# Four Strassen units instead of three in two column pairs of a decoder trunk

## The chip, the cores and the metric

The kernel runs on one core of a Trainium2 chip. The metric is device time in microseconds. The core has TensorE (PE) for matmuls, VectorE (DVE), ScalarE (ACT), GpSimd (POOL) and SyncE (SP), which issues nearly all DMAs. Each engine works through its own instructions in a fixed order and waits on the others through semaphores.

## The reference

One layer of a decoder trunk over 256 tokens of width 2048, all in fp32. It is nine large projections with element-wise work and a short recurrence between them:

```
u = rmsnorm(x) @ W_in               # 2048 -> 12288: c, b, xa, za, q, f, iv, og (1024 each), ga, gb (2048 each)
ya = b * conv3(c * xa) * silu(za)
yb = rmsnorm(hgrn2(silu(q), f, iv)) * silu(og)      # gated linear recurrence, 8 heads of 128
m = sigmoid(ga) * (ya @ W_a) + sigmoid(gb) * (yb @ W_b)
x = x + m @ W_o                                     # 2048 -> 2048
x = x + sigmoid(rmsnorm(x) @ W_pg) * (p @ W_pp)     # 2048 -> 2048
out = rmsnorm(x)
```

## The kernel before

**Splits.** A matmul in full precision is made of three in a faster rounded format (fp32r): each operand is the sum of a rounded part "hi" and the rest "lo", and hi·hi + hi·lo + lo·hi is accumulated. The weights are streamed from memory. For each part of 128 rows x 1024 columns of the stream, SP loads `raw` (`load_raw`, three buffers of two parts, 1 MB each), ACT writes `whi` = raw rounded (L166) and DVE `wlo` = raw − whi (L167). This is `split`. So ACT, DVE and PE each pass over the whole weight stream once. The activations are the stationary operand: for each 128 rows of them and each half of the tokens PE loads 128x128 and streams 512 columns of weights.

**Groups, pairs and programs.** A column group is 512 columns wide. Most groups run alone, in eight steps of two 128-row blocks; a step is 12 matmuls. Six pairs of groups run together by a program, a list of units `(u, c)`, where `c` names a chunk of 256 rows of the contraction. `(0, c)` or `(1, c)` is two chunks of one group, `(2, c)` one chunk of both: two parts, 24 matmuls. `("S", c)` is one chunk of both groups by a Strassen scheme, seven products instead of eight: 21 matmuls. It has four parts, three of 1024 columns and one of 512. Behind its part 0, `combine_weights` makes sums and differences of the weights on DVE: L181 (128x1024), L184 and L185 (128x512). Part 1 is the split of the 512-wide sum `t2`. The activations need sums of their own, the forms (`forms`, L777 to L785), made earlier: those of the second half's pair by `forms_of_x` out of a fresh load of x, those of the last gate pair in `ep_o`, behind the transposition of x.

The pairs that matter here are `VG` (program `INNER`: value `iv` and output gate `og` of the second half of the heads) and `GP` (program `LATE`: the second and third group of W_pg). `OUT` is the program of the first two groups of W_o; the third and fourth run alone as `O` (j = 2, 3). Then come the first W_pg group (`PG`, 0), `GP`, and the last one (`PG`, 3).

**What sets the order.** The program is written step by step, and each engine keeps the order in which its instructions were written, except that a scheduler may move one forward by its own estimate of times. `tc.issue_after` forbids this: an instruction under it stays behind the named one on its engine. The main loop splits ahead of PE by `ahead(pos)` parts: three, some more where extra buffers are open (`MORE`), and up to five more in the tail. In between it runs the epilogues, generators that do one piece of work at each `yield` (`advance`, `step`); the pieces stand behind the last splits (`state["splits"]`). In the ranges `inner` and `tied` the splits too stand behind the last split.

**Transpositions.** `turned` turns a block of 256 tokens x 512 columns: four DMAs write it to memory (`turn`, L346), one reads it back (L350), and after `lag` yields DVE transposes its 32x32 squares (L354). `ep_o` does so with each 512 columns of x: an addition of the matmul's result (L845), two copies on ACT (L947), the DMAs, the squares for the norm (L954), the transposition, and for j ≥ 2 four `put` (L310 on ACT and L311 on DVE, hi and lo of the turned block). PE needs the blocks in the first W_pg group: the last one, j = 3, in its seventh step. `ep_f` makes the recurrence's decay of one half of the heads: two sigmoids on ACT (L400, L402), four operations of DVE on 256 columns (L407), four more for the keys (L414), logarithms on ACT that need a table load (L424), a scan on DVE (L434). Its second half runs beside `VG`.

PSUM has banks of two sets, "g" and "s"; `bank` takes the next of a set.

Of the kernel before, what the change touches and what calls it, by code (L numbers as in the profile page):

```python
# [10 lines left out]
F32R = mybir.dt.float32r  # L11
# [4 lines left out]
P = 128  # L16
T = 256
# [23 lines left out]

GATES = ("S", 0), (0, 2), ("S", 1), (1, 2), ("S", 4), (0, 6), ("S", 5), (1, 6)
OPENING = (0, 2), (0, 4), ("S", 0), (0, 6), ("S", 1), (1, 2), (1, 4), (1, 6)
INNER = (0, 4), ("S", 0), (0, 6), ("S", 1), (2, 3), ("S", 2), (1, 4), (1, 6)
FRONT = (0, 2), (0, 4), (0, 6), ("S", 0), (1, 2), ("S", 1), (1, 4), (1, 6)
OUT = (0, 4), ("S", 0), (1, 4), ("S", 1), (2, 3), ("S", 2), (0, 6), (1, 6)
LATE = (0, 4), ("S", 0), (0, 6), ("S", 1), (2, 3), ("S", 2), (1, 4), (1, 6)


PRM_GMIX, PRM_GPLE, PRM_GHG, PRM_LB, PRM_CONV = 0, 16, 32, 40, 48  # L50
# [5 lines left out]
def hybrid_kernel(ctx, tc, xT, x, pT, prm, gfin, masks, w_in, w_a, w_b, w_o, w_pg, w_pp, out):  # L56
# [195 lines left out]
    closing = last_unit("OO", OUT)  # L252
    last = range(gates[-1] + 1, closing + 1)
    outer = range(closing + 6, of_kind("O")[-1] + 1)
    tied.append(range(last[0] - 4, outer[-1] + 1))
    inner = [of_kind(kind) for kind in ("QV", "VG")]
    inner = range(inner[0][0] - 3, inner[0][-1] + 1), range(inner[1][0] - 6, inner[1][-1] + 1)

# [44 lines left out]
    def put(op, k, src, scale=None):  # L303

        hi, lo = op[0][:, k, :], op[1][:, k, :]
        if scale is None:
            nc.scalar.activation(out=hi, in_=src, func=AF.Copy)
            nc.vector.tensor_tensor(out=lo, in0=src, in1=hi.bitcast(F32), op=ALU.subtract)
        else:
            nc.scalar.activation(out=hi, in_=src, func=AF.Identity, scale=scale)  # L310
            nc.vector.scalar_tensor_tensor(  # L311
                out=lo, in0=src, scalar=scale, in1=hi.bitcast(F32), op0=ALU.mult, op1=ALU.subtract
            )


    def rsqrt_of(ss, n, width, tag):
# [20 lines left out]
    def turned(src, lag, dst=None):  # L337

        d = dram.tile([P, 4, T], F32, tag="turn", bufs=3, name=nm("turn"))
        to = d.rearrange("(b i) a x -> a i b x", b=4)
        for a in range(4):
            state["sent"] = nc.sync.dma_start(  # L346
                out=to[a], in_=src[32 * a : 32 * a + 32, :].rearrange("i (b x) -> i b x", b=4)
            ).ins
        yield
        nc.sync.dma_start(out=src, in_=d.rearrange("p a x -> p (a x)"))  # L350
        for _ in range(lag):
            yield
        dst = t4() if dst is None else dst
        nc.vector.transpose(  # L354
            out=dst.rearrange("p (k a e) -> p a k e", a=4, e=32), in_=src.rearrange("p (a k e) -> p a k e", a=4, e=32)
        )
        return dst
# [37 lines left out]
    def ep_f(j, psum):  # L395
# [8 lines left out]
        one, low = (state[n][:, j * 4 : j * 4 + 4] for n in ("oml", "lbm"))  # L404
        for h in range(4):
            s = slice(h * T, (h + 1) * T)
            nc.vector.tensor_scalar(  # L407
                out=sg[:, s], in0=sg[:, s], scalar1=one[:, h : h + 1], scalar2=low[:, h : h + 1],
                op0=ALU.mult, op1=ALU.add,
            )  # L410
# [5 lines left out]
            )  # L416
        yield
        yield


        lf, last = t4(), sc(8, "lfl", 2)
        lv, fv = segments(lf), segments(sg)
# [518 lines left out]
    def ep_o(j, psum):  # L941
        xs = state["x"]
        x1 = t4()
        for t in range(NT):
            d = xs[:, t, j * CW : (j + 1) * CW]
            add(d, d, psum[t])
            nc.scalar.activation(out=spread(x1, t), in_=blocks(d), func=AF.Copy)  # L947
        turn = turned(x1, 6 if j == 1 else 2)
        next(turn)
        yield  # L950
        junk = t4()
# [18 lines left out]
            yield from forms("x1T", form_tiles(pools["tmp3"], f"So{j}", len(chunks)), r, chunks)  # L970
            return
        for c in range(4):
            put(state["x1T"], j * 4 + c, x1[:, c * T : (c + 1) * T], gain(PRM_GPLE, j * 4 + c))
        if j == 3:
            tot = sc(2, "tot2", 1)
            nc.vector.tensor_reduce(
# [342 lines left out]
    for pos, (gi, c) in enumerate(steps[:last_group]):  # L1319
# [31 lines left out]
            step(active[-1])  # L1351
        if pos == inner[1][0] - 8:
            third = [
                pools["branch"].tile([P, 1024], F32R, tag=f"ybT{x}1", bufs=1, name=nm("form"))[:, :512] for x in "hl"
            ]
            active.append(forms_of_x((2,), lambda n: lambda: third))
            step(active[-1])
        if 0 <= pos - NORM < 4:
            add_squares(pos - NORM)
# [40 lines left out]
                load_projection(1 + c[0] // 2)  # L1400
            continue
        if c == 0:
            psum = [bank("s" if kind == "PP" and j > 1 else "g") for _ in range(NT)]
        hi, lo = parts.pop(pos)
        for i in range(2):
            k = 2 * c + i
# [134 lines left out]
```

## Time and profile before

| | |
|---|---|
| median of 3 runs | 807.91 us (807.77 to 809.03) |
| the profiled execution | 809.07 us, its span 807.3 |
| PE busy | 798.0 us, 99% |
| DVE busy | 685.1 us, 85% |
| ACT busy | 492.1 us, 61% |
| POOL busy | 95.4 us, 12% |
| DMA | 191.20 MB, mean 237 GB/s |
| PE's clock | 0.9 or more of full speed in all slices but the last |

The trace is of one execution. A row of a timeline gives the start in us from the span's start, the duration (of the whole run of instructions, where there are several: x3), the engine, the line, the operation, output and inputs without buffer numbers, and in brackets how long the engine had been idle and what ended it. A matmul's row is longer than the time it holds PE, because matmuls overlap; what counts is from start to start. "Ready" of a part is the end of its L167.

In the kernel after the change the lines from ep_f on are numbered up to seven higher: L354 becomes L355, L407's place on ACT is L409, L947 becomes L954, L954 becomes L961, L1017 becomes L1024, L1258 and L1280 become L1265 and L1287.

### The profile page before, as it was taken

To read this page: it belongs to the slowest core of one execution; us is meant where nothing else is said; L and a number is where in the kernel's file an instruction comes from. 1 tells how busy PE (TensorE), PEld (TensorE's weight loads), DVE (VectorE), ACT (ScalarE), POOL (GpSimd) and SP (SyncE) were. 2 spreads that over 40 slices of the span, in tenths; PEclk is the share of its full clock that TensorE was granted. 3 is DMA by queue.
4 is the path that set the end of the run, shared out by engine and by line. 5 is a ranking of instruction groups with operands and counts; after the bars stand their busy time and mean duration, and the time that the engine had idled before them with its cause. 6 is when DMAs were issued, how large, how long until landed. Compare 5 with 4: busy or idle time off the path is not lost.

```text
span 807.3 us, 11113 instructions
## 1 busy us (share of the span) xinstructions
PE 798.0 (99%) x4169; PEld 662.3 (82%) x4169; DVE 685.1 (85%) x798; ACT 492.1 (61%) x662; POOL 95.4 (12%) x74
## 2 busy tenths in 40 slices
PE   9999999999999999999999999999999999999995
PEld 7888888888888888888888888888888888887885
DVE  5968897966779987978998998998998988859995
ACT  6967565575656665586674564564565556746562
POOL 0000145300000054300001000000100000002032
PEclk9999999999999999999999999999999999999998
DMA  9899855747676755667584775775875669877542
GB/s 345 295 335 319 268 174 203 237 167 241 240 261 190 261 183 201 209 211 257 189 307 158 227 275 171 239 264 179 275 266 196 208 246 348 327 236 281 205 173 104
DMA packets 50309, 191.20 MB, mean 237 GB/s; under 512 B 5712, under 2 KB 15184, under 8 KB 36304
## 3 DMA queue, kind: packets, MB, share of 16 engines
q1 hardware_dynamic: 50112, 190.24, 68.4%
q8 instruction: 32, 0.52, 0.2%
q10 hardware_dynamic: 144, 0.26, 0.1%
q14 instruction: 21, 0.17, 0.1%
HBM read 175.80 MB, written 14.68 MB: 236 GB/s over the span
## 4 chain that ended last, share of the span: by engine, by line
PE 82%; DVE 10%; issue 2%; DMA 2%; ACT 2%; SPq 0%; POOL 0%; ACTq 0%; POOLq 0%; DVEq 0%
PE g L1258 48%; PE g L1280 25%; PE s L1280 6%; DVE wlo L167 5%; DMA raw<-in_w_pg 2%; ACT whi L166 1%; DVE raw L181 1%; DMA raw<-in_w_o 1%; PE s L1258 1%; PE s L504 1%; DVE t L845 1%; PE s L1131 1%; DVE t L184 1%; DVE t L1017 0%; DVE t L354 0%
## 5 line engine op out<-in xcount | busy, mean ns | idle before, releaser
L167 DVE TENSOR_TENSOR wlo<-raw,whi 128x1024 fp32r<-128x1024 f32 (+1 forms) x320 | 390.2, 1243 | 92.2 <-ACT whi L166 89.4
L166 ACT ACTIVATE whi<-raw 128x1024 fp32r<-128x1024 f32 (+1 forms) x320 | 325.8, 1047 | 175.8 <-PE g L1258 98.3
L1258 PE MATMUL g<-whi,xl 128*128 128x512 f32 (+1 forms) x464 | 177.1, 382 | 0.3 <-DVE xl L311 0.3
L1258 PE MATMUL g<-whi,xh 128*128 128x512 f32 (+1 forms) x464 | 177.4, 383 | 0.0
L1258 PE MATMUL g<-wlo,xh 128*128 128x512 f32 (+1 forms) x464 | 177.1, 382 | 0.0
L1280 PE MATMUL g<-whi,xl 128*128 128x512 f32 x316 | 122.9, 389 | 0.0
L1280 PE MATMUL g<-wlo,xh 128*128 128x512 f32 x316 | 122.9, 389 | 0.0
L1280 PE MATMUL g<-whi,xh 128*128 128x512 f32 x316 | 122.6, 389 | 0.0
L1258 PEld LDWEIGHTS g<-whi,xl 128*128 128x128 f32 x464 | 87.2, 188 | 17.6 <-DVE xl L311 0.8
L1258 PEld LDWEIGHTS g<-whi,xh 128*128 128x128 f32 x464 | 87.2, 188 | 17.0 <-ACT xh L310 0.3
L1258 PEld LDWEIGHTS g<-wlo,xh 128*128 128x128 f32 x464 | 87.3, 188 | 16.8
L166 ACT ACTIVATE whi<-t 128x512 fp32r<-128x512 f32 x25 | 15.8, 632 | 92.1 <-DVE t L184 92.1
L1280 PEld LDWEIGHTS g<-whi,xl 128*128 128x128 f32 x316 | 59.3, 188 | 12.4
L1280 PEld LDWEIGHTS g<-whi,xh 128*128 128x128 f32 x316 | 59.3, 188 | 12.3
L1280 PEld LDWEIGHTS g<-wlo,xh 128*128 128x128 f32 x316 | 59.3, 188 | 12.3
L927 POOL TENSOR_TENSOR t<-ga,gb 128x512 f32<-128x512 f32 x6 | 10.6, 1790 | 188.0 <-issue 118.1
L181 DVE TENSOR_TENSOR raw<-raw 128x1024 f32<-128x1024 f32 x25 | 31.5, 1261 | 0.6
L1258 PE MATMUL g<-whi,yaTh 128*128 128x512 f32 (+1 forms) x74 | 28.2, 388 | 0.0
L1258 PE MATMUL g<-wlo,yaTh 128*128 128x512 f32 (+1 forms) x74 | 27.9, 383 | 0.0
L1258 PE MATMUL g<-whi,yaTl 128*128 128x512 f32 (+1 forms) x74 | 27.9, 383 | 0.0
L1258 PE MATMUL g<-whi,mh 128*128 128x512 f32 x64 | 24.8, 391 | 0.1
L1258 PE MATMUL g<-whi,ml 128*128 128x512 f32 x64 | 24.9, 389 | 0.0
(309 smaller groups left out, 1117.0 us busy)
## 6 DMA issues: line engine op xcount, KB each, us to landing
raw<-in_w_in SPq DMA_DIRECT2D x68, 1024.0 KB, 5.0
raw<-in_w_in SPq DMA_DIRECT2D x37, 512.0 KB, 5.1
raw<-in_w_o SPq DMA_DIRECT2D x12, 1024.0 KB, 6.5
raw<-in_w_pg SPq DMA_DIRECT2D x12, 1024.0 KB, 6.4
raw<-in_w_in SPq DMA_DIRECT2D x38, 256.0 KB, 5.1
turn<-t SPq DMA_DIRECT2D x72, 128.0 KB, 2.8
t<-turn SPq DMA_DIRECT2D x18, 512.0 KB, 5.2
raw<-in_w_a SPq DMA_DIRECT2D x8, 1024.0 KB, 5.6
```

The costliest lines, as they stand in the source:

```text
L166: a = nc.scalar.activation(out=hi[:, s], in_=src[:, s], func=AF.Copy)
L167: v = nc.vector.tensor_tensor(out=lo[:, s], in0=src[:, s], in1=hi[:, s].bitcast(F32), op=ALU.subtract)
L181: nc.vector.tensor_tensor(out=b[:, 0:4:3, :], in0=b[:, 0:3:2, :], in1=b[:, 3:4, :].to_broadcast([P, 2, CW]), op=ALU.subtract)
L184: nc.vector.tensor_tensor(out=t2, in0=b[:, 2, :], in1=b[:, 0, :], op=ALU.add)
L504: nc.tensor.matmul(heads(bk)[r, h, c if at is None else slice(at, at + 32)], key(h)[:, r], query(h)[:, c], start=True, stop=True, tile_pos ...
L845: nc.vector.tensor_tensor(out=out, in0=x, in1=y, op=ALU.add)
L927: (nc.vector if j == 3 else nc.gpsimd).tensor_tensor(out=spread(m, t), in0=blocks(ga[:, s]), in1=blocks(gb[:, s]), op=ALU.add)
L1131: nc.tensor.matmul(wb[:m, :n], *ones, start=True, stop=True)
L1258: nc.tensor.matmul(psum, a, b, start=first and n == 0, stop=last and n == 2)
L1280: nc.tensor.matmul(banks[name], x, y[:, s], start=k == total[name] and i == 0, stop=k == 1 and i == 2)
```

## The change

```diff
-INNER = (0, 4), ("S", 0), (0, 6), ("S", 1), (2, 3), ("S", 2), (1, 4), (1, 6)
+INNER = (0, 4), ("S", 0), (0, 6), ("S", 1), (1, 4), ("S", 2), ("S", 3), (1, 6)
-LATE = (0, 4), ("S", 0), (0, 6), ("S", 1), (2, 3), ("S", 2), (1, 4), (1, 6)
+LATE = (0, 4), ("S", 0), (0, 6), ("S", 1), (1, 4), ("S", 2), ("S", 3), (1, 6)
...
-    tied.append(range(last[0] - 4, outer[-1] + 1))
+    tied.append(range(last[0] - 4, late + 10))
...
     def put(op, k, src, scale=None):
-            nc.scalar.activation(out=hi, in_=src, func=AF.Identity, scale=scale)
-            nc.vector.scalar_tensor_tensor(
+            a = nc.scalar.activation(out=hi, in_=src, func=AF.Identity, scale=scale)
+            v = nc.vector.scalar_tensor_tensor(
...
+            return a.ins, v.ins
...
     def ep_f(j, psum):
         for h in range(4):
             s = slice(h * T, (h + 1) * T)
+            if j:
+                nc.scalar.activation(
+                    out=sg[:, s], in_=sg[:, s], func=AF.Identity, scale=one[:, h : h + 1], bias=low[:, h : h + 1]
+                )
+                continue
             nc.vector.tensor_scalar(
...
         yield
         yield
+        if j:
+            yield
...
     def ep_o(j, psum):
-        turn = turned(x1, 6 if j == 1 else 2)
+        turn = turned(x1, (2, 6, 6, 4)[j])
...
-            put(state["x1T"], j * 4 + c, x1[:, c * T : (c + 1) * T], gain(PRM_GPLE, j * 4 + c))
+            state["splits"] = put(state["x1T"], j * 4 + c, x1[:, c * T : (c + 1) * T], gain(PRM_GPLE, j * 4 + c))
...
-                pools["branch"].tile([P, 1024], F32R, tag=f"ybT{x}1", bufs=1, name=nm("form"))[:, :512] for x in "hl"
+                pools["branch"].tile([P, 1024], F32R, tag=f"ybT{x}1", bufs=1, name=nm("form")) for x in "hl"
             ]
-            active.append(forms_of_x((2,), lambda n: lambda: third))
+            active.append(forms_of_x((2, 3), lambda n: lambda: third))
...
-            psum = [bank("s" if kind == "PP" and j > 1 else "g") for _ in range(NT)]
+            psum = [bank("s" if kind == "PP" and j > 1 or kind == "O" and j == 2 else "g") for _ in range(NT)]
```

1. In `INNER` and `LATE` the unit `(2, 3)` becomes `("S", 3)`. It stands directly behind `("S", 2)`, and `(1, 4)` moves ahead of both. Everywhere in the kernel before a Strassen unit has another kind of unit ahead of it.
2. The forms for chunk 3: `forms_of_x` makes two chunks at once, and the forms of the second quarter of x in `ep_o` (j = 1) become 1024 wide, since `chunks` there is read from `LATE`.
3. In `ep_f`, for the second half, the four L407 become activations on ACT, and the logarithms come one step later.
4. The transpositions of x wait 2, 6, 6 and 4 steps (before: 2, 6, 2, 2); the four `put` of j = 2 and 3 become part of `state["splits"]`, and the tied range reaches ten parts into the first W_pg group. So the splits there stand behind the puts, and in written order.
5. The third W_o group takes banks of the set "s".

On DVE, in VG, from the end of the unit `(2, 3)` over S2 on (`raw_2355` is S2's tile, `wlo_2433` its part 0). Before:

```order
L167 TENSOR_TENSOR wlo_2433<-raw_2355,whi_2432 128x1024
L181 TENSOR_TENSOR raw_2355<-raw_2355 128x2x512
L184 TENSOR_TENSOR t_416_2436<-raw_2355 128x512
L185 TENSOR_TENSOR raw_2355<-raw_2355,t_416_2436 128x512
L167 TENSOR_TENSOR wlo_2446<-t_416_2436,whi_2445 128x512
L167 TENSOR_TENSOR wlo_2456<-raw_2355,whi_2455 128x1024
L167 TENSOR_TENSOR wlo_2466<-raw_2355,whi_2465 128x1024
L167 TENSOR_TENSOR wlo_2482<-raw_2419,whi_2481 128x1024
L167 TENSOR_TENSOR wlo_2501<-raw_2419,whi_2500 128x1024
L167 TENSOR_TENSOR wlo_2511<-raw_2443,whi_2510 128x1024
```

After, with S2's tile `raw_2357` and S3's `raw_2421`:

```order
L167 TENSOR_TENSOR wlo_2437<-raw_2357,whi_2436 128x1024
L181 TENSOR_TENSOR raw_2357<-raw_2357 128x2x512
L184 TENSOR_TENSOR t_416_2440<-raw_2357 128x512
L185 TENSOR_TENSOR raw_2357<-raw_2357,t_416_2440 128x512
L167 TENSOR_TENSOR wlo_2450<-t_416_2440,whi_2449 128x512
L167 TENSOR_TENSOR wlo_2460<-raw_2357,whi_2459 128x1024
L167 TENSOR_TENSOR wlo_2470<-raw_2357,whi_2469 128x1024
L167 TENSOR_TENSOR wlo_2487<-raw_2421,whi_2486 128x1024
L181 TENSOR_TENSOR raw_2421<-raw_2421 128x2x512
L184 TENSOR_TENSOR t_427_2490<-raw_2421 128x512
L185 TENSOR_TENSOR raw_2421<-raw_2421,t_427_2490 128x512
L167 TENSOR_TENSOR wlo_2509<-t_427_2490,whi_2508 128x512
```

Three splits of parts stand between the two blocks of additions. In GP the same happens, save that part 3 is split ahead of part 1.

On ACT, where the last quarter of x is copied for its transposition (the copies are L947 before, L954 after; the squares L954, then L961). Before:

```order
L166 ACTIVATE whi_6288<-raw_6158 128x1024
L310 ACTIVATE xh_5825<-t_1103_6183,prm_t 128x256 x4
L947 ACTIVATE t_1114_6273<-xs 128x4x4x32
L954 ACTIVATE t_1120_6306,ss_1036_5822<-xs 128x512
L947 ACTIVATE t_1114_6273<-xs 128x4x4x32
L954 ACTIVATE t_1120_6306,ss_1036_5822<-xs 128x512
L166 ACTIVATE whi_6310<-raw_6237 128x1024
L166 ACTIVATE whi_6328<-raw_6237 128x1024
```

After:

```order
L310 ACTIVATE xh_5838<-t_1115_6258,prm_t 128x256 x4
L166 ACTIVATE whi_6268<-raw_6171 128x1024
L166 ACTIVATE whi_6301<-raw_6171 128x1024
L166 ACTIVATE whi_6323<-raw_6240 128x1024
L166 ACTIVATE whi_6341<-raw_6240 128x1024
L954 ACTIVATE t_1119_6286<-xs 128x4x4x32 x2
L961 ACTIVATE t_1125_6319,ss_1041_5835<-xs 128x512 x2
L166 ACTIVATE whi_6357<-raw_6284 128x1024
```

Four splits moved ahead of the copies. On SP's queue at the same place, where `turn` is that quarter on its way out and the load with `turn` as its source its way back. Before:

```order
L346 DMA turn_6278<-t_1114_6273 32x4x256 x4
L131 DMA raw_6326<-in_w_pg 128x2048
L350 DMA t_1114_6273<-turn_6278 128x1024
L119 DMA raw_6376<-in_w_pg 128x1024
L121 DMA raw_6376<-in_w_pg 128x512 x2
L1209 DMA pw_6396<-kept_224 128x1024
```

After:

```order
L1216 DMA pw_6409<-kept_224 128x1024
L131 DMA raw_6339<-in_w_pg 128x2048
L347 DMA turn_6291<-t_1119_6286 32x4x256 x4
L119 DMA raw_6373<-in_w_pg 128x1024
L121 DMA raw_6373<-in_w_pg 128x512
L351 DMA t_1119_6286<-turn_6291 128x1024
L121 DMA raw_6373<-in_w_pg 128x512
```

A load of 1 MB moved ahead of the four transfers, and most of the next tile's load ahead of the way back.

## The prediction

> **What bounds the kernel.** I read the page's first part, then the waits of PE, then the timelines of PE and DVE around the two pairs whose program changes.
>
> ```profile
> PE 798.0 (99%) x4169; PEld 662.3 (82%) x4169; DVE 685.1 (85%) x798; ACT 492.1 (61%) x662; POOL 95.4 (12%) x74
> ```
>
> ```profile
> PE g L1258 <- DVE xl L311: 0.3, 1, 0.3
> ```
>
> PE is the bound: it is busy 99% of a span of 807.3 us, and the waits view shows one wait of 0.3 us for another engine. So time can go only with matmuls, or come with new waits on split weights. The waits view hides small ones, because a row of PE lasts 0.39 us and rows overlap; a wait shows as a start that comes more than 0.227 us after the last one. That pitch is read below between 267.14 and 267.37. Three places have more.
>
> The first is inside S2 of the second half's pair (VG). These are PE's starts there, and DVE's rows:
>
> ```profile
> 266.01 0.39 PE L1280 MATMUL s<-wlo,xh 128*128 128x512 f32 x1
> 267.14 0.39 PE L1280 MATMUL s<-whi,form 128*128 128x512 f32 x1
> 267.37 0.39 PE L1280 MATMUL s<-wlo,form 128*128 128x512 f32 x1
> 268.05 0.39 PE L1280 MATMUL g<-whi,xh 128*128 128x512 f32 x1
> 268.46 0.50 PE L1280 MATMUL g<-whi,form 128*128 128x512 f32 x1
> 268.80 0.39 PE L1280 MATMUL s<-whi,form 128*128 128x512 f32 x1
> ```
>
> ```profile
> 261.26 2.32 DVE L167 TENSOR_TENSOR wlo<-raw,whi 128x1024 fp32r<-128x1024 f32 x2
> 263.61 1.22 DVE L181 TENSOR_TENSOR raw<-raw 128x1024 f32<-128x1024 f32 x1
> 264.87 0.69 DVE L184 TENSOR_TENSOR t<-raw 128x512 f32<-128x512 f32 x1
> 265.59 0.69 DVE L185 TENSOR_TENSOR raw<-raw,t 128x512 f32<-128x512 f32 x1
> 266.34 0.69 DVE L167 TENSOR_TENSOR wlo<-t,whi 128x512 fp32r<-128x512 f32 x1
> 267.50 5.76 DVE L167 TENSOR_TENSOR wlo<-raw,whi 128x1024 fp32r<-128x1024 f32 x5 [0.46 <-ACT whi L166]
> ```
>
> 268.05 to 268.46 is 0.41 and 268.46 to 268.80 is 0.34, so S2 loses 0.18 + 0.11 = 0.29 us. The reader is to see why: S2's part 0 is ready at 263.58 (261.26 + 2.32), 2.43 us ahead of its use at 266.01; part 1 is ready at 267.03 and used at 267.37, 0.34 ahead. The three additions of a Strassen unit have eaten the lead. The second and third places come with their parts below.
>
> **Six Strassen products fewer.** VG and the last gate pair (GP) each swap a unit of 24 matmuls for one of 21: 3 x 0.227 = 0.68 us less of PE in each, 1.36 in all. This is certain, as PE has no idle time that would take it back.
>
> **VG, the price of two neighbours.** Each Strassen unit now has DVE's three additions behind its part 0, and no plain unit stands between S2 and S3. From S2's part 0 to S3's part 0 DVE needs: additions and the half split, 263.58 to 267.03, 3.45; the whole split behind ACT, to 267.50 + 1.15 = 268.65, 1.62 to 1.70; two more at 1.15 (5.76 / 5). That is 7.4 us for a unit that PE eats in 21 x 0.227 = 4.76. To S3's part 1 it is 7.4 + 3.45 = 10.85 us, and PE wants that part 21 + 6 matmuls after S2's part 0, 6.12 us. The lead falls by 4.73; there are 2.43 us of it, plus what the rest of the change gives ahead of S2. Part 2 is then late by 0.37 more: it follows part 1 by 1.70 on DVE, by 1.33 on PE once S2's 0.29 is taken off (part 2's lo is used at about 269.0).
>
> What the change gives ahead of S2 is the four L407 operations moved to ACT.
>
> ```profile
> 236.85 0.41 DVE L407 TENSOR_SCALAR t<-t,lc,lc 128x256 f32<-128x256 f32 x1
> 237.18 1.22 DVE L181 TENSOR_TENSOR raw<-raw 128x1024 f32<-128x1024 f32 x1
> 247.05 3.50 DVE L167 TENSOR_TENSOR wlo<-raw,whi 128x1024 fp32r<-128x1024 f32 x3 [1.36 <-ACT whi L166]
> 243.52 1.28 ACT L424 ACT_TABLE_LOAD   x1
> 713.59 1.71 ACT L310 ACTIVATE xh<-t,prm_t 128x256 fp32r<-128x256 f32 x4
> ```
>
> One costs DVE 0.33 (236.85 to 237.18), four 1.3: that is the upper end of the gain. The lower end is nothing, as DVE already waits 1.36 at 247.05 for ACT, which has loaded a table (1.28) between two splits, and ACT now has four instructions more ahead of that. Following both rows of instructions, ACT's four (estimated at 0.43 each, 1.71 / 4, from the same form in the tail) hold the half split of S0 back by 0.6, and the table load still stands ahead of the fifth split. I find S2's part 0 ready 0.4 earlier, nearer the lower end, and take 0.4. So VG stalls 4.73 - 2.43 - 0.4 + 0.37 = 2.3 us; net, with S2's 0.29 gone and 0.68 fewer: 2.3 - 0.29 - 0.68 = **+1.3** (bounds: 0.4 with the whole 1.3, 1.7 with nothing). The plain unit and the epilogues behind it refill the lead.
>
> The wider form (one DMA more, forms of 1024 instead of 512) costs DVE a split of 1.22 instead of 0.69 and four additions twice as wide, some 1 us by the rows above, and ACT as much. It lies some 10 us ahead of this row:
>
> ```profile
> 232.21 2.36 DVE L167 TENSOR_TENSOR wlo<-raw,whi 128x1024 fp32r<-128x1024 f32 x2 [4.90 <-ACT whi L166]
> ```
>
> DVE stands idle for 4.90 in one go before VG, so I cost it at nothing. If that cover were gone, it would come off the lead of S2. The wider form in the output groups is costed the same way.
>
> **The bank of O's third group.** Its first matmul waits for a bank of the set that the pair ahead of it still occupies.
>
> ```profile
> 669.12 0.39 PE L1258 MATMUL g<-whi,ml 128*128 128x512 f32 x1
> 669.58 0.50 PE L1258 MATMUL g<-whi,mh 128*128 128x512 f32 x1
> ```
>
> 0.46 instead of 0.23, and 0.11 behind it: 0.34 us. The other set of banks is free by then. I take **-0.34** (between 0 and that).
>
> **The tail.** Call T0 the first matmul of the first w_pg group (712.55). In it PE loses time where it needs the last quarter of x, transposed:
>
> ```profile
> 712.55 0.39 PE L1258 MATMUL g<-whi,xh 128*128 128x512 f32 x1
> 730.46 0.39 PE L1280 MATMUL g<-wlo,xh 128*128 128x512 f32 x1
> 730.78 0.50 PE L1258 MATMUL g<-whi,xh 128*128 128x512 f32 x1
> 731.12 0.39 PE L1258 MATMUL g<-wlo,xh 128*128 128x512 f32 x1
> 732.04 0.40 PE L1280 MATMUL g<-whi,xh 128*128 128x512 f32 x1
> 732.79 0.73 PE L1258 MATMUL g<-whi,xl 128*128 128x512 f32 x2 [0.35 <-DVE xl L311]
> ```
>
> 0.09 + 0.11 + 0.52 and 0.11 behind the last: 0.83 us. The order now puts that quarter's transposition (L355) and the four L311 ahead of two splits on DVE, but its copies out of x behind four splits on ACT, and its four transfers behind a load of 1 MB on SP's queue. Before, its chain ran so:
>
> ```profile
> 715.21 0.62 ACT L947 ACTIVATE t<-xs 128x512 f32<-128x512 f32 x1
> 717.60 3.90 ACT L166 ACTIVATE whi<-raw 128x1024 fp32r<-128x1024 f32 x4
> L346 SPq DMA_DIRECT2D turn<-t x4: 325/438/446, 717.1 to 718.4; - x4
> 722.24 0.34 SPq L350 DMA_DIRECT2D t<-turn  x1
> 728.86 1.24 DVE L354 STREAM_TRANSPOSE t<-t 128x1024 f32<-128x1024 f32 x1
> DMA to landing us min/median/max: 2.1/3.8/5.6
> raw<-in_w_pg SPq DMA_DIRECT2D x12, 1024.0 KB, 6.4
> ```
>
> In the new order three splits run from T0 (3 x 0.98), the copies take 1.1, so the transfers start at T0 + 4.1 and the last is issued at 5.5 (before, the first at 717.1, T0 + 4.6, and the last at 718.4). Landing takes 3.8 as before (718.4 to 722.24), then 5.6 back: X, the start of the transposition, is T0 + 15.0 (before T0 + 16.31). Bounds: 13.7, with the shortest and the median landing, and 16.3, no better than before. PE needs the quarter at T0 + 16.3; a transposition of 1.2 and the first of four conversions fit to within some tenths.
>
> From X on DVE never waits long, and its rows add up. Before:
>
> ```profile
> 745.23 2.20 DVE L181 TENSOR_TENSOR raw<-raw 128x1024 f32<-128x1024 f32 x1
> 747.47 1.67 DVE L184 TENSOR_TENSOR t<-raw 128x512 f32<-128x512 f32 x1
> 751.52 4.62 DVE L167 TENSOR_TENSOR wlo<-raw,whi 128x1024 fp32r<-128x1024 f32 x4
> 742.48 6.10 POOL L1026 TENSOR_TENSOR xs<-xs,gfin_t 128x512 f32<-128x512 f32 x2 [18.46 <-ACT t L1019]
> 761.24 0.39 PE L1280 MATMUL s<-wlo,xh 128*128 128x512 f32 x1
> ```
>
> S2's part 0 is ready at 751.52 + 4.62 = 756.14, 27.28 after the transposition; the new order has one split more between: 28.4. Then S2 to S3's part 0, 7.35 (as in VG), and to S3's part 2, whose split stands behind that of part 3, 1.25 + 0.72 + 0.61 + 1.14 + 0.60 + 1.14 = 5.5: X + 41.2, or T0 + 56.2. PE, without waits, would use S2's part 0 at 761.24 - 0.83 = T0 + 47.86, S3's 4.76 later, and its part 2 nine matmuls (2.04) on: T0 + 54.66. PE is 1.6 us late in all by then (0 at X = 13.4; 2.9 at 16.3). Net: 1.6 - 0.83 - 0.68 = **+0.1**. Behind S3 the plain units give DVE its lead back.
>
> The 41.2 holds two additions that ran long while POOL worked: 2.20 and 1.67 against 1.22 and 0.69 in VG, 1.96 in all. The Trainium skill, SBUF — State Buffer, "Who interferes with whom", says that a VectorE instruction with two SBUF inputs and a GpSimd one that reads SBUF take one port as a lock, and that the later one blocks for the whole instruction. By that rule up to 2 x 3.05 us would go, 4.1 more than the rows show. The rows show 0.98 each, and the sum goes by them.
>
> **Sum.** 1.3 - 0.34 + 0.1 = +1.1 us. The profiled execution took 809.07 (span 807.3 and what lies around it), the median of the runs is 807.91; the sum is a difference, and set on the median it gives 809.0. Its own bounds are 806.5 (VG 0.4, tail -1.5, bank -0.34: -1.4) and 811.0 (VG 1.7, tail 1.4, bank 0: +3.1). I count 0.2%, 1.6 us, as what can be told from no change.
>
> **Rivals.**
> *A, the lead holds.* If ACT's delays ahead of S2 fall away and DVE is more than 1 us further ahead in VG, and X is early, only savings stay: -1.36 - 0.29 - 0.34 - 0.83 = -2.8, 805.1; with one small stall 805.9. For it: DVE is busy 85% of the span, and waits 1.36 and 0.46 in rows above that a better order could fill. Against: the 10.85 of DVE against 6.12 of PE leaves 2.3 us to find. Chance 0.24.
> *B, the last quarter comes later.* Its four transfers now stand behind a load of 1 MB, and each us on X is a us of the end. From X = T0 + 15.6 on the kernel is slower by over 1.6; at 17.0 it is +3.1, 811.0. For it: the load would be issued at about T0 + 3.2, when the second split frees its buffer, and such a load takes 6.4 by the row above; transfers that move only behind it land at 9.6 or later, and 5.6 back make X 15.2 to 16. Against: they are ready 0.5 earlier than before. The Trainium skill, DMA: Bandwidth & Descriptors, "Queues, rings and completion order", has each ring consumed in order, which is this rival's mechanism; no run yet shows these transfers behind a load. Chance 0.22.
> *C, POOL's two products block whole instructions of DVE.* In the new order they start beside splits instead of additions; at 3.05 us each (6.10 / 2) they cost 4.1 more: 813.1. The rows above speak against it. Chance 0.05.
> *D, one of the two stalls only.* S3 stalls in VG but not in the tail: 1.3 - 0.34 - 1.5 = -0.5, 807.4. Chance 0.04.
>
> **How the numbers follow.** The forecast has 0.45, of which a quarter (0.12) lies above 809.5 and the rest within. Faster: A, 0.24. Slower: 0.12 + B 0.22 + C 0.05 = 0.39. Same: 0.33 + D 0.04 = 0.37. The range reaches down to A with a small stall, 805.6, and up beyond B, 812.0; what lies outside is the best part of A and C. The forecast's own range is 806.5 to 811.0.
>
> **What would show it.** PE rows: 6 matmuls fewer, a start 1.5 to 2 us late at S3's part 1 in VG with DVE's half split as releaser, none at S2. DVE: two blocks of additions with three splits between, no wait longer than 0.5 in the second. No 0.46 at the third O group. In the tail the transposition at T0 + 14 to 16, a late start of PE in S3 of GP. The prediction fails if VG's S3 waits less than 1 us (my 0.4 was too small), or if X is outside 13.7 to 16.3.

## The result

The changed kernel takes 817.03 us (815.85 to 817.27), the kernel before in the same runs 808.05 (807.77 to 809.03): a ratio of 1.0103, 95% interval 1.0091 to 1.0115. The forecast was 809.0, no change that can be told, with a range up to 812.0; the result lies outside. The profiled execution has a span of 815.5 us, 8.2 more than before.

The waits of PE, after (us in total, times, longest):

```profile
PE g L1265 <- ACT xh L310: 3.1, 1, 3.1
PE s L1287 <- ACT whi L166: 1.1, 1, 1.1
...
PE g L1265 <- DVE t L852: 0.4, 1, 0.4
PE g L1265 <- DVE v L852: 0.4, 1, 0.4
...
PE s L1287 <- DVE wlo L167: 0.2, 1, 0.2
```

There are three kinds. The second and the last of these rows are S3 of the second half's pair. Its PE and DVE timelines:

```profile
271.96 0.39 PE L1287 MATMUL g<-whi,xl 128*128 128x512 f32 x1
273.46 0.49 PE L1287 MATMUL s<-whi,form 128*128 128x512 f32 x1 [1.11 <-ACT whi L166]
274.19 0.50 PE L1287 MATMUL s<-wlo,form 128*128 128x512 f32 x1 [0.23 <-DVE wlo L167]
274.99 0.39 PE L1287 MATMUL g<-whi,xh 128*128 128x512 f32 x1
275.55 0.50 PE L1287 MATMUL g<-whi,form 128*128 128x512 f32 x1 [0.16 <-ACT whi L166]
```

```profile
262.05 1.21 DVE L167 TENSOR_TENSOR wlo<-raw,whi 128x1024 fp32r<-128x1024 f32 x1
...
267.18 3.50 DVE L167 TENSOR_TENSOR wlo<-raw,whi 128x1024 fp32r<-128x1024 f32 x3 [0.46 <-ACT whi L166]
270.71 1.23 DVE L181 TENSOR_TENSOR raw<-raw 128x1024 f32<-128x1024 f32 x1
...
273.44 0.69 DVE L167 TENSOR_TENSOR wlo<-t,whi 128x512 fp32r<-128x512 f32 x1
```

From start to start, less 0.227 each, S3 loses 1.27 + 0.50 + 0.11 + 0.33 + 0.11 = 2.32 us. Part 0 of S2 is ready at 263.26, 0.32 earlier than before; as PE's starts stand 0.28 later in this trace (its use is at 266.29, before at 266.01), the lead over PE is 3.03 instead of 2.43. Part 1 of S3 is ready at 274.13, 10.87 behind part 0 of S2. S2's own 0.29 us are gone, and so is the wait at the third W_o group.

The second kind waits for a bank. The group behind each of the two pairs writes a bank that the pair's last additions (L852) have to empty first:

```profile
285.20 0.39 PE L1265 MATMUL g<-whi,xl 128*128 128x512 f32 x1
286.00 0.50 PE L1265 MATMUL g<-whi,xh 128*128 128x512 f32 x1 [0.41 <-DVE v L852]
783.22 0.39 PE L1287 MATMUL g<-whi,xl 128*128 128x512 f32 x1
784.05 0.50 PE L1265 MATMUL g<-whi,xh 128*128 128x512 f32 x1 [0.45 <-DVE t L852]
```

0.57 + 0.11 and 0.61 + 0.11: 0.68 and 0.72 us. Neither is in the trace of before.

The third and largest is where PE needs the last quarter of x, in the first W_pg group. T0 is now 714.54.

```profile
730.64 0.39 PE L1265 MATMUL g<-whi,xl 128*128 128x512 f32 x1
734.15 0.80 PE L1265 MATMUL g<-whi,xh 128*128 128x512 f32 x1 [3.12 <-ACT xh L310]
734.75 0.63 PE L1265 MATMUL g<-wlo,xh 128*128 128x512 f32 x1
735.17 0.63 PE L1265 MATMUL g<-whi,xl 128*128 128x512 f32 x1
```

PE stands still for 3.29 us more than its pitch, and then its pitch is 0.43 instead of 0.227. The windows of PE (length, busy with its count, granted clock, DMA share, GB/s) show why; the granted clock is the share of full speed at which TensorE runs:

```profile
715.00:730.00 15.00, 15.00 (x68) 1.00 0.73 242
730.00:734.00 4.00, 1.03 (x5) 0.94 0.98 354
734.00:740.00 6.00, 5.85 (x14) 0.50 0.41 140
740.00:745.00 5.00, 5.00 (x23) 0.96 0.54 197
```

The trace's clock record has 0.50 from 733.5 to 740.4, 6.8 us, of which PE has work in 6.2. The wait (with 0.37 behind its first matmul) is 3.65, the slow matmuls cost 13 x 0.2 = 2.6: PE is 6.3 us late by 740. In the gate pair no Strassen unit waits any more.

The quarter's chain, in the order of its steps:

```profile
713.95 1.71 ACT L310 ACTIVATE xh<-t,prm_t 128x256 fp32r<-128x256 f32 x4 [2.63 <-DVE t L355]
715.57 3.89 ACT L166 ACTIVATE whi<-raw 128x1024 fp32r<-128x1024 f32 x4
719.36 1.14 ACT L954 ACTIVATE t<-xs 128x512 f32<-128x512 f32 x2
720.23 0.33 SPq L131 DMA_DIRECT2D raw<-in_w_pg  x1
720.60 2.40 SPq L347 DMA_DIRECT2D turn<-t  x4
728.18 0.33 SPq L351 DMA_DIRECT2D t<-turn  x1
732.31 1.25 DVE L355 STREAM_TRANSPOSE t<-t 128x1024 f32<-128x1024 f32 x1 [6.96 <-DMA t<-turn]
```

ACT stood idle 2.63 us for the third quarter's transposition, did its puts (L310) and four splits, and reached the copies only at T0 + 4.8. The transfers went out behind the load of 1 MB, and the transposition began at T0 + 17.77.

Against the 8.2 us of the two spans: VG 2.32 - 0.29 - 0.68 = +1.35; the two banks +1.40; O's bank -0.34; the tail 6.25 - 0.83 - 0.68 = +4.74; behind the last matmul, where the last pieces of the sum of squares now stand in another order, +0.7 (9.03 us from the start of the last matmul to the end, before 8.35; with the old program of the gate pair, in experiment 3, it is 8.21, and more was not taken apart). That is 7.85; most of the rest stands at the front, as PE's start at 177 us is already 0.28 later.

### The profile page after: what moved, and what is told of

It reads as the page before. It is cut to its first block, busy times and chain, and to the rows that moved or that the text cites. A ratio compares the mean times of both kernels' runs of the same rounds, so it can differ in the third digit from the quotient of the medians.

```text
span 815.5 us, 11122 instructions
## 1 busy us (share of the span) xinstructions
PE 800.1 (98%) x4162; PEld 663.3 (81%) x4163; DVE 695.4 (85%) x804; ACT 498.9 (61%) x672; POOL 93.0 (11%) x74
## 5 line engine op out<-in xcount | busy, mean ns | idle before, releaser
L167 DVE TENSOR_TENSOR wlo<-raw,whi 128x1024 fp32r<-128x1024 f32 (+1 forms) x322 | 394.9, 1251 | 84.2 <-ACT whi L166 82.8
L1287 PE MATMUL g<-whi,xl 128*128 128x512 f32 x304 | 118.3, 389 | 0.0
L1287 PE MATMUL g<-wlo,xh 128*128 128x512 f32 x304 | 118.3, 389 | 0.0
L1287 PE MATMUL g<-whi,xh 128*128 128x512 f32 x304 | 118.1, 389 | 0.0
L181 DVE TENSOR_TENSOR raw<-raw 128x1024 f32<-128x1024 f32 x27 | 34.0, 1259 | 0.7
L355 DVE STREAM_TRANSPOSE t<-t 128x1024 f32<-128x1024 f32 x16 | 19.8, 1237 | 7.0 <-DMA t<-turn 7.0
L1265 PE MATMUL g<-whi,ybTh 128*128 128x512 f32 x64 | 24.9, 389 | 0.0
```

What stands on the lines that cost most here:

```text
L167: v = nc.vector.tensor_tensor(out=lo[:, s], in0=src[:, s], in1=hi[:, s].bitcast(F32), op=ALU.subtract)
L181: nc.vector.tensor_tensor(out=b[:, 0:4:3, :], in0=b[:, 0:3:2, :], in1=b[:, 3:4, :].to_broadcast([P, 2, CW]), op=ALU.subtract)
L355: nc.vector.transpose(out=dst.rearrange("p (k a e) -> p a k e", a=4, e=32), in_=src.rearrange("p (a k e) -> p a k e", a=4, e=32))
L1265: nc.tensor.matmul(psum, a, b, start=first and n == 0, stop=last and n == 2)
L1287: nc.tensor.matmul(banks[name], x, y[:, s], start=k == total[name] and i == 0, stop=k == 1 and i == 2)
```

## The experiments

The theory after the result: the order around the first W_pg group (puts, tied range, lags) makes the last quarter late, and the end of the tail follows from when that quarter's transposition starts; that two Strassen units are neighbours costs the second half's pair 2.3 us and a bank. Rivals: the loss in the tail is the slow clock's own; or four Strassen units are too many wherever they stand. All ratios below are against the kernel before in the same runs (808.2 to 808.8).

### 1. The puts out of the order

```diff
-            state["splits"] = put(state["x1T"], j * 4 + c, x1[:, c * T : (c + 1) * T], gain(PRM_GPLE, j * 4 + c))
+            put(state["x1T"], j * 4 + c, x1[:, c * T : (c + 1) * T], gain(PRM_GPLE, j * 4 + c))
```

> As the changed kernel, but the puts of the last quarters of x are not part of what the splits stand behind. The order then has the copies of the last quarter ahead of two more splits on ACT, its four transfers ahead of the 1 MB load on SP, and ten matmuls of the gate pair moved into the first W_pg group, as before. Theory (order): the wait of 3.65 us in the first W_pg group goes, and with it the slow clock behind it (2.6 us); the small waits of before come back (0.83) and the gate pair's fourth Strassen unit gets later, up to 2.9 instead of 0.72: 812 to 814 us. Rival (clock by itself): the slow clock behind that place is not tied to the wait, and stays: 814.5 to 816.5, with TensorE at half clock near 735 us. Rival (adjacency alone): the loss is in the neighbouring Strassen units, and it stays within 1 us of 817.

811.35 us, ratio 1.0038 (1.0027 to 1.0050). 5.7 us of the loss go with this one line (5.3 by the ratios); the wait and the slow clock go together, and the 0.83 us do not come back. The order is again that of before: copies ahead of the last splits, transfers ahead of the load, ten of the gate pair's matmuls moved into the wait. The time is 0.7 under the expected range: no wait comes in the gate pair's S3, though the transposition is no earlier than in the kernel before (728.84 against 728.86), because T0 is 2.1 later:

```profile
728.84 1.24 DVE L355 STREAM_TRANSPOSE t<-t 128x1024 f32<-128x1024 f32 x1
```

The bank wait behind the pair is 1.1 here.

### 2. The second half's pair as before

```diff
-INNER = (0, 4), ("S", 0), (0, 6), ("S", 1), (1, 4), ("S", 2), ("S", 3), (1, 6)
+INNER = (0, 4), ("S", 0), (0, 6), ("S", 1), (2, 3), ("S", 2), (1, 4), (1, 6)
...
-            active.append(forms_of_x((2, 3), lambda n: lambda: third))
+            active.append(forms_of_x((2,), lambda n: lambda: third))
```

> As the changed kernel, with the program of the second half's pair and its forms as before. Theory (adjacency costs 2.3 us there, of which 0.68 and 0.29 come back, and 0.68 more behind it): about 2.0 us off, 815.0, no wait over 0.2 us in that pair. Rival (the operations moved to ACT cost the lead there, not the neighbours): the waits stay, 817.5.

812.56 us, 1.0045 (1.0030 to 1.0060): 4.5 off, where 2.0 were expected. No wait is left in that pair, as the theory says; S2's 0.29 is gone too, so the operations on ACT and the other parts do help there. But the tail gains as well, 400 us later. The first block of x is written out earlier than in the changed kernel: the first `turn` on SP's queue stands at the same time as in the kernel before. Before, this kernel and the changed one:

```profile
672.55 1.79 SPq L346 DMA_DIRECT2D turn<-t  x4
```

```profile
672.60 1.79 SPq L347 DMA_DIRECT2D turn<-t  x4
727.54 1.25 DVE L355 STREAM_TRANSPOSE t<-t 128x1024 f32<-128x1024 f32 x1 [6.91 <-DMA t<-turn]
769.27 0.50 PE L1287 MATMUL s<-wlo,So1h 128*128 128x512 f32 x1 [0.69 <-DVE wlo L167]
770.40 0.50 PE L1287 MATMUL s<-wlo,So1h 128*128 128x512 f32 x1 [0.17 <-DVE wlo L167]
```

```profile
677.10 1.77 SPq L347 DMA_DIRECT2D turn<-t  x4
```

The new program in VG makes PE's T0 2.7 us later (711.80 to 714.54), but the chain of x's blocks 4.5 later, and the last transposition 4.8 (727.54 to 732.31). With the old program the wait in the first W_pg group is 1.26 (1.37 with the matmul behind it), no slow clock follows, and DVE is late for S0, S1 and S3 of the gate pair instead, 2.55 in all.

### 3. The last gate pair as before

```diff
-LATE = (0, 4), ("S", 0), (0, 6), ("S", 1), (1, 4), ("S", 2), ("S", 3), (1, 6)
+LATE = (0, 4), ("S", 0), (0, 6), ("S", 1), (2, 3), ("S", 2), (1, 4), (1, 6)
```

> As the changed kernel, with the program of the last gate pair as before. Theory (the wait ahead of it, in the first W_pg group, comes from the order of puts, splits and copies, not from the program): the wait of 3.3 us and the half clock stay; 0.72 us of waits in that pair go and 0.68 of matmuls come: 817.0 within 0.5. Rival (the fourth unit causes the tail's loss): about 6 us off, 811.

815.7 us, 1.0085 (1.0070 to 1.0100): 1.3 off, 0.8 more than the theory's bound allows, and far from the rival's 6. PE is idle for 4.6 here until the last quarter comes (733.12 is the transposition), with the half clock behind it. The wait does not come from the fourth unit.

### 4. A plain unit between the third and the fourth

```diff
-INNER = (0, 4), ("S", 0), (0, 6), ("S", 1), (1, 4), ("S", 2), ("S", 3), (1, 6)
+INNER = (0, 4), ("S", 0), (0, 6), ("S", 1), (1, 4), ("S", 2), (1, 6), ("S", 3)
```

and `LATE` likewise.

> As the changed kernel, with the last two units of both programs exchanged, so that a plain unit stands between the third and the fourth Strassen unit. Same work. Theory: DVE has 4.8 + 5.4 us of matmuls for its 10.9 us instead of 6.1, the waits of 2.3 us in the second half's pair fall under 0.3, the tail's stay: 814 to 815. Rival (four units are too many for DVE in any order): the wait only moves to the fourth unit, 816 to 817.5.

826.8 us, 1.0219 (1.0202 to 1.0237): the theory's 814 to 815 and the rival's 816 to 817.5 both missed by far. The waits at S3 in VG do go: between 177 and 280 us PE's starts show none. What it brings instead is idle time behind the pairs. PE in the recurrence behind VG, at the wait of the first W_pg group and at the end of the gate pair:

```profile
354.60 0.32 PE L511 MATMUL s<-qT,kT 128*32 128x32 f32 x2 [3.93 <-issue]
354.85 0.80 PE L1265 MATMUL g<-whi,xh 128*128 128x512 f32 x1
...
737.93 0.50 PE L1265 MATMUL g<-whi,xh 128*128 128x512 f32 x1 [2.65 <-ACT xh L310]
738.27 0.40 PE L1265 MATMUL g<-wlo,xh 128*128 128x512 f32 x1
...
785.35 0.39 PE L1287 MATMUL s<-whi,So1l 128*128 128x512 f32 x1
791.51 0.80 PE L1265 MATMUL g<-whi,xh 128*128 128x512 f32 x1 [5.76 <-DVE t L852]
```

A Strassen unit writes seven of the eight banks of its pair. With it last, the additions that empty them start only when the pair ends, and the group behind the gate pair waits 5.76 us. The 3.93 us in the recurrence end 0.2 us behind three additions on DVE (L852), but the profile names no releaser there, so that they too are a wait for banks is not shown. Behind both the granted clock is 0.50 for 6.8 us. So the place of the last Strassen unit has two sides: close behind the third it comes ahead of DVE, and close to the pair's end it holds the banks.

### 5. The idle time filled

```diff
+        if kind == "PG" and j == 0 and c == 6:
+            idle = bank("s")
+            ones = [nc.const_aps.tensor(1.0, [P, i], mybir.dt.bfloat16) for i in (P, CW)]
+            for _ in range(14):
+                tc.keep_in_program_order(nc.tensor.matmul(idle, *ones, start=True, stop=True))
```

> As the changed kernel, with 14 matmuls of constants into a free bank (about 3 us of TensorE work whose result nothing reads) ahead of the seventh step of the first W_pg group, where TensorE waits 3.3 us for the last quarter of x. Theory (the slow clock comes from the idle time): the quarter arrives when it did, but TensorE goes on at full clock, the 13 matmuls at 0.43 us are gone, 2.6 us off: 814.4 within 0.7, no half clock near 735 us. Rival (the slow clock has another cause, such as the load of the stretch ahead): it stays, 816.5 to 818.

817.29 us, 1.0112 (1.0097 to 1.0126): the same time as the changed kernel, and yet the clock did not fall in the wait. Over the whole execution its mean is 0.996 or 0.997 in all four executions, as in the kernel before; in those of the changed kernel it is 0.992 to 0.995. PE's timeline, its window, DVE's transposition and the end of S3:

```profile
731.18 3.01 PE L1416 MATMUL s<-const-bfloat16-1.0 128*128 128x512 bf16 x13
735.29 0.50 PE L1265 MATMUL g<-whi,xh 128*128 128x512 f32 x1 [1.10 <-ACT xh L310]
```

```profile
734.00:740.00 6.00, 4.89 (x21) 1.00 0.36 147
```

```profile
733.45 1.25 DVE L355 STREAM_TRANSPOSE t<-t 128x1024 f32<-128x1024 f32 x1 [8.02 <-DMA t<-turn]
776.31 0.50 PE L1287 MATMUL s<-wlo,So1h 128*128 128x512 f32 x1 [0.17 <-DVE wlo L167]
```

So the slow clock does come from the idle time: with TensorE busy there is none. But its 2.6 us are not a loss of their own. At full clock PE reaches S0, S1 and S3 of the gate pair earlier and waits there for DVE, 2.55 us in all, the same waits as in experiment 2. The transposition was also 1.1 us later in this execution, the slowest of the four (819.03); from it to the last wait of S3 it is 42.86 us here and 42.86 in experiment 2. What sets the end is DVE's row of work behind that transposition. In the changed kernel that part is ready at 775.10 and used at 775.51, 0.41 us apart:

```profile
773.88 5.76 DVE L167 TENSOR_TENSOR wlo<-raw,whi 128x1024 fp32r<-128x1024 f32 x5
775.51 0.39 PE L1287 MATMUL s<-wlo,So1h 128*128 128x512 f32 x1
```

The slow clock filled the time that DVE needed.

### 6. Puts out of the order and the second half's pair as before

The changes of experiments 1 and 2 together.

> As the kernel without the puts in the splits' order, with the program of the second half's pair as before too. What is left of the change is the last gate pair's fourth unit, the bank of the third W_o group, the four operations on ACT and the lags. Theory (the terms of the trace add): 2.0 us under the kernel with only the puts undone, 807.3 to 809.3, and by the rows 0.3 (bank) + 0.4 (tail) better than before. Rival (the puts' order and the first half's lead are tied to each other by the timing of loads): a new wait of over 1 us shows in the first W_pg group, 810 or more.

810.36 us, 1.0022 (1.0013 to 1.0031): 1.0 under experiment 1, half of what was expected, and slower than before, not faster. The trace is of the slowest of its ten executions (811.47), so it shows where time is lost and not how much the median loses. The loss is in the tail: the last transposition starts at the same time as in experiment 1, but T0 is 2.5 earlier (712.10).

```profile
728.80 1.24 DVE L355 STREAM_TRANSPOSE t<-t 128x1024 f32<-128x1024 f32 x1
769.14 0.50 PE L1287 MATMUL s<-wlo,So1h 128*128 128x512 f32 x1 [0.18 <-DVE wlo L167]
```

The waits are 1.22 in the first W_pg group and 1.24 at S3. In three kernels with the old order (before, experiments 1 and 6) the transposition stands at 728.80 to 728.86, behind a split whose load had just landed, while T0 ranges from 712.1 to 714.6. That load sets it: in these three and in experiments 8, 9 and 11, which have that order too, it lands between 725.0 and 726.6, and the transposition starts 2.25 to 2.26 us later in all six. Why it lands within 0.1 us of one time in the three is not settled. What experiments 1 and 6 show is that a wait ahead of T0 and a wait behind it are not two costs, since the first gives the chain time.

### 7. No neighbours, and a plain unit last

```diff
-INNER = (0, 4), ("S", 0), (0, 6), ("S", 1), (1, 4), ("S", 2), ("S", 3), (1, 6)
+INNER = ("S", 0), (0, 4), ("S", 1), (0, 6), ("S", 2), (1, 4), ("S", 3), (1, 6)
```

and `LATE` likewise, with the puts out of the order.

> As the kernel without the puts in the splits' order, with both programs in the order S0, plain, S1, plain, S2, plain, S3, plain: no two Strassen units adjacent, and a plain unit last. Theory: the 2.3 us of waits in S3 of the second half's pair go, and so do most of the 0.7 and 1.1 us for banks behind the pairs, since the last Strassen unit is as early as the plain unit behind it allows or earlier: 808 or less, unless starting with a Strassen unit waits for its banks. Rival (four units in a pair are more than DVE's lead bears): waits of 2 us or more move to the last Strassen unit or behind the pair, 811 or more.

812.89 us, 1.0055 (1.0040 to 1.0070): 1.5 over experiment 1. The rival's time holds, though not its place. In VG the waits are 0.4 us in S1, 0.9 in the plain unit behind it, 1.9 in S2 and 0.1 in S3, 3.3 in all, where the neighbours cost 2.3; the bank wait behind VG stays (0.9). In the gate pair it is gone, and 1.5 us of waits stand in the pair instead. So the loss needs no neighbours. An estimate of the shortage from the rows: over the pair DVE has 4 x 7.4 us for Strassen units, 4 x 2.3 for plain ones and, by the rows of the kernel before, 2.3 for the scan, 1.2 for a transposition, 1.1 for the keys and 1.3 for the products of q: about 45, where PE has 4 x 4.76 + 4 x 5.44 = 41. It is not the only reading of this run: DVE also waits 2.29 us for ACT in S1, and the scan stands behind that, ahead of most of the waits.

### 8 to 11. Each part alone

The kernel before with only the program of VG and its forms (8), with only that of GP (9), with only the order, that is puts, tied range and lags (10); and the changed kernel with both programs as before and the puts out of the order (11), so that the operations on ACT, the bank of the third W_o group, the lags and the tied range are left of the change. Of (10), against the kernel before:

```diff
-    tied.append(range(last[0] - 4, outer[-1] + 1))
+    tied.append(range(last[0] - 4, late + 10))
...
-        turn = turned(x1, 6 if j == 1 else 2)
+        turn = turned(x1, (2, 6, 6, 4)[j])
-            put(state["x1T"], j * 4 + c, x1[:, c * T : (c + 1) * T], gain(PRM_GPLE, j * 4 + c))
+            state["splits"] = put(state["x1T"], j * 4 + c, x1[:, c * T : (c + 1) * T], gain(PRM_GPLE, j * 4 + c))
```

> The kernel before, with only the program of the second half's pair changed (and its forms). Theory (DVE's lead): without the operations moved to ACT the waits at S3 are 0.4 longer than the 2.3 us of the changed kernel, 0.7 more at the bank behind the pair, 1.0 comes back; T0 is some 2.4 later, which gives the last quarter of x time and takes the 0.83 us of waits in the first W_pg group: 808.5 + 1.5 = 810. Rival (parts add without such relief): 811.

809.33 us, 1.0012 (1.0003 to 1.0022). The waits at S3 are 1.41, less than the 2.7 expected, 0.69 at the bank, and the 0.83 us in the first W_pg group are gone. Between theory and no change. So the four operations on ACT and the later logarithms, which are left out here, do not help beside the new program: without them S2's part 0 is ready 3.94 us ahead of its use, with them 3.03. ACT's table load begins at 241.72 here and at 244.22 in the changed kernel, and DVE waits 1.37 and 2.29 us for ACT behind it.

> The kernel before, with only the program of the last gate pair changed (and the wider forms). Theory: a wait of 1.2 at S3, 1.1 for the bank behind the pair, 0.68 of matmuls less: 808.5 + 1.7 = 810.2. Rival (only the neighbours' wait, the bank wait comes from the puts' lags): 809.1.

809.92 us, 1.0020 (1.0011 to 1.0030). 1.14 us of waits at S3, 0.99 at the bank: as expected.

> The kernel before, with only the order around the first W_pg group changed: the puts in the splits' order, the tied range, the lags. Theory (the last quarter's copies stand behind four splits, its transfers behind a load of 1 MB): a wait of 1 to 4 us in the first W_pg group, and waits in the gate pair's Strassen units behind it: 809.5 to 812. Rival (the order is harmless without the fourth units): 808 to 808.8.

809.65 us, 1.0018 (1.0008 to 1.0029), at the lower end. The ten executions spread from 808.12 to 811.66, and the one with the trace is among the faster (808.74, with a span 0.3 shorter than that of the kernel before), so the trace does not show where the median loses its 1.4. In it there is no wait in the first W_pg group. DVE's two transpositions show why:

```profile
706.42 1.24 DVE L355 STREAM_TRANSPOSE t<-t 128x1024 f32<-128x1024 f32 x1
726.15 1.25 DVE L355 STREAM_TRANSPOSE t<-t 128x1024 f32<-128x1024 f32 x1 [5.44 <-DMA t<-turn]
```

The third quarter is turned 5.5 us ahead of T0 (711.88), so its puts are done and the copies of the last quarter are not held; the last quarter comes at T0 + 14.27. In the changed kernel the third quarter comes 1.9 ahead of T0 and the last at T0 + 17.77.

> The changed kernel with both programs as before and the puts not in the splits' order: the four operations on ACT, the bank of the third W_o group, the lags and the tied range are left. Theory: 0.34 us for the bank, the rest within noise: 808.1. Rival (the operations on ACT cost the second half's pair its splits): a wait over 0.3 us there and 809 or more.

808.35 us, 1.0002 (0.9993 to 1.0011): nothing that can be told, as expected. No wait in VG, none at the third W_o group.

Alone, the parts cost 1.1, 1.7, 1.4 and 0.1 us against the runs of before, 4.2 by the ratios, though (10) and (11) share the lags and the tied range. Together they cost 8.3 by the ratio.

### 12. The lags of the last two transpositions

```diff
-        turn = turned(x1, (2, 6, 6, 4)[j])
+        turn = turned(x1, (2, 6, 2, 2)[j])
```

> As the changed kernel, with the lags of the third and fourth transposition at 2 as before. The third one's puts then stand two splits earlier, the copies of the last quarter still behind four splits and its transfers behind two loads of 1 MB. Theory (the last quarter's chain starts late because the copies stand behind splits that stand behind the third quarter's puts, which wait for its late transposition): the copies start up to 2 us earlier, the wait in the first W_pg group is 1 to 2 us instead of 3.3, no half clock, waits in the gate pair's units as with the constants' matmuls (2.5 us): 814 to 816. Rival (the queue of loads alone makes the quarter late): no change, 817.

819.0 us, 1.0131 (1.0115 to 1.0148): slower still, so both sides missed. The trace is of the fastest execution (818.05). The copies begin at 719.61, no earlier, since six splits now stand ahead of them. The transfers are issued at 720.77 to 722.10, about as in the changed kernel, but the load of 1 MB that stood just ahead of them there now stands behind them; they are out 3.7 us after the last issue instead of 5.7, and the transposition begins 1.5 earlier (730.80). So the place of that load is worth some 2 us of the way out. The wait in the first W_pg group is 2.3 us, with 0.8 more soon behind it, and the clock stays full in this execution. It did not in all: two of the others have a mean of 0.992, as the traced execution of the changed kernel has. Two more splits now stand on DVE behind the transposition, and PE gets S3's third part 45.1 us after it instead of 42.9. 1.5 us of waits at the group's start come on top.

## Why the prediction was wrong

**Right.** VG: the stall was put at 2.3 us and measured 2.32, with 10.87 us of DVE's work against the 10.85 of the sum. The 1.36 us of matmuls and the 0.34 of O's bank came as costed. That the 2.3 is met so closely is in part luck. The sum took 0.4 us of lead from the four operations on ACT and nothing from the new program; the lead grew by 0.60, and by experiment 8 the new program alone gives 1.51, of which the operations on ACT take 0.91 back. With the old program (experiment 11) they cost nothing that can be told. Why the new program alone gives so much was not found. Rival C did not come: the two additions beside POOL's products took as long as before.

```profile
751.20 2.19 DVE L181 TENSOR_TENSOR raw<-raw 128x1024 f32<-128x1024 f32 x1
753.43 1.67 DVE L184 TENSOR_TENSOR t<-raw 128x512 f32<-128x512 f32 x1
```

The sum was right to go by 0.98 each, and 3.05 was no price of a product: POOL's first product starts 2.75 us ahead of L181 in the kernel before, 3.69 in the changed one and 2.10 in experiment 1, and ends 1.12 behind L181's start in all three, so most of its span is waiting, and the rows fit a block of DVE for 0.98 us by each product.

**The step that failed** is the start of the last quarter's transposition: "X, the start of the transposition, is T0 + 15.0", with bounds of 13.7 and 16.3. It was 17.77, and 18.82 in the trace of experiment 5, whose program is the same up to there. The steps behind that number were "three splits run from T0", transfers from T0 + 4.1 to 5.5, 3.8 out and 5.6 back. Measured: four splits from T0 + 1.03, behind puts that waited for the third quarter; transfers from T0 + 6.06 to 7.96; 5.7 out, behind the load; 4.1 back. This is rival B (0.22), beyond the price that I worked out for it: I had X no later than T0 + 17.0. (The lower bound of 13.7 does not come out of its rows: 5.5 + 2.1 + 5.6 is 13.2. Nothing hangs on it.)

What the working lacked is that VG and the tail are not separate. The sum took the third quarter's turn as done before T0. The trace of experiment 10 shows that this is so when the order alone changes (X at T0 + 14.3), experiment 2 that it still nearly holds with the gate pair's fourth unit (15.7). Only with VG's new program does the chain of x's blocks slip by 4.5 us against 2.7 of PE, and then the puts hold the splits, the splits the copies, and the copies and a load the transfers. In experiment 8, with that program alone, the first block is already turned 2.6 us later than before and T0 is 0.9 later. How VG's program delays that chain by more than PE was not found; from there on all parts of the stream stand two places later in the rotation of buffers, but no run tells that apart.

**The second term that was mis-sized** is DVE's work from there to S3's third part, 41.2; measured 42.8 to 42.9. One us of it stands right behind the transposition in the changed order: the four L311 wait 0.6 for ACT's first L310, and the next split 0.46 for ACT. The form of the sum held: X and 42.86 give the last wait of S3 in experiments 2 and 5, the two kernels with these lags and the new order whose S3 waits, and in the changed kernel the part is ready 0.41 us ahead of its use.

**Left out.** The banks behind the pairs, 0.68 + 0.72: "The plain unit and the epilogues behind it refill the lead" looked at DVE's lead alone, and not at who waits for the epilogue. Moving the last Strassen unit one unit later moves the additions that empty the banks. Also 0.7 us behind the last matmul, where the order of the epilogue's last pieces moved.

**Right in part.** The chance of slower, 0.39, was mostly hung on a larger X, and that is what happened; but "each us on X is a us of the end" was meant from T0 + 15.6 up and gives +3.9 at 17.77 with the sum's other terms. With 42.9 instead of 41.2, the banks and the end it gives 7.6, worked out after the result.

## What to carry to other kernels

When an order is tied, follow each chain that crosses it from the first instruction that it now waits for, and take that one's time from a trace in which all the parts of the change are together, not part by part: here parts that cost 1 to 2 us alone cost 8 together. Here a stage with a lead of 0.3 us took no further unit without a wait in any of the three orders tried, so count the engine's work over the whole stage before looking at neighbours. And before crediting a slow clock or a wait with its whole length, ask what would have been waited for next; here, filling the wait showed that the next wait took the same microseconds.

## What the runs showed of the hardware

The granted clock of TensorE fell to 0.50 after idle times of 3.12 us (changed kernel), 3.93 and 5.76 (experiment 4) and 4.63 (experiment 3), and not after 2.65 (experiment 4) or 2.2 (experiment 12). The clock records have it there for 6.83 us in the changed kernel and in both places of experiment 4, and for 3.41 in experiment 3; in experiment 3 it fell 0.4 us after PE had work again. 6.83 is twice 3.41. The Trainium skill, TensorE: Matmul & The Clock Gate, "Part 1: The HAM clock gate (the "warmup" mystery)", says that the clock halves after an idle window of about 3.4 us and is whole again after a busy one of that length. The runs agree on the half. On the way down they differ: an idle time of 3.12 us was enough. On the way back they agree: in all four cases the clock is whole again at the end of the first stretch of 3.41 us, counted from the fall, in which PE had work throughout. I had not weighed it in the prediction, as no wait in it came near 3 us.

The four transfers of 128 KB landed 2.1 to 3.6 us after their issue where no load was in flight ahead of them (experiment 1) and 5.6 to 6.4 where a load of 1 MB, issued 0.4 us ahead, was (changed kernel); there the first landed 0.4 us after that load. This is what the prediction drew from the Trainium skill, DMA: Bandwidth & Descriptors, "Queues, rings and completion order", and had only as a rival.
